# GpSimd normalises two of four tiles, late passes and selection move, and the odd layer's values follow two heads' scores later

## The chip, the cores and the metric

The kernel runs on one core of one Trainium2 chip. The metric is the device time of one execution in microseconds (us), given as the median of several runs. The rows below come from one profiled execution. The engines are named as the profile names them: PE (TensorE, matmuls), PEld (its weight loads), DVE (VectorE), ACT (ScalarE), POOL (GpSimd) and SP (SyncE, which issues most DMAs).

## The reference, cut to what matters

Three blocks act one after the other on 512 tokens of width 1024, in float32.

```
h = rms_norm(x, mix_norm_g)
u, q, k, v, f_logit, g_ssm, g_att = split(h @ w_in)
merged = sigmoid(g_ssm) * s5_branch(u, ...) + sigmoid(g_att) * forgetting_attention(q, k, v, ...)
x = x + merged @ w_out
h2 = rms_norm(x, ffn_norm_g)
x = x + peer_ffn(h2, ...)   # top 16 experts of 16384 per token and head: gelu(h.u) * gate, times v
# even layer: rmsnorm, dsa_mixer (an index scores keys, top_k keeps 128 per token) beside diff_mixer (4 heads), output product
x = x + swiglu(rmsnorm(x, g0), w_gate0, w_up0, w_down0)
# odd layer: rmsnorm, nsa_mixer (16 heads in 4 groups, compressed, selected and windowed keys), output product
x = x + swiglu(rmsnorm(x, g1), w_gate1, w_up1, w_down1)
# diff_mixer, one head:
a = softmax(q0 k0) - lam * softmax(q1 k1);  o = rmsnorm(a @ v) * gain
```

## The kernel before, in words

The 512 tokens are four tiles of 128 rows (`NT = 4`); the width is eight blocks of 128 (`KD = 8`). Each float32 operand is split into a high part and a remainder, and each product is three matmuls, high by high, high by remainder, remainder by high (`mm3`, L332 to L334).

Weights pass through one ordered stream of 1024-column blocks (`Stream`, L56 to L95). A block is loaded by SP into `wraw` (three buffers), its high part `whi` is made by ACT (L75), its remainder `wlo` by DVE (L81); for the names in `ADDED` the remainder is made by an ACT copy of minus w (L78) and a POOL DMA that adds w (L79).

`norm_T` (L323 to L326) makes each normalised tile `xn` on DVE, transposes it on PE into `tx` or `ax`, and ACT and DVE split that into `hhi` and `hlo`. `proj_T` multiplies a weight block by all 512 tokens; `proj_256` gives 256 output columns for each tile.

The stages run in this order, by the profiled execution's time: start norm, `u`, forget gates and the fox attention with the S5 branch in the background (0 to 282 us), gates and output (to 469), norm and peer queries with the top 16 (to 530), the peer passes (530 to 1767), the even layer's norm and index (to 1862), four diff heads with the selection of keys (to 2013), eight latent heads with the output product (to 2126), ffn0 (to 2500), the odd layer (2500 to 2900), ffn1 (to the end). In the peer part there are 128 passes over u and 128 over v. The first `N_SPILL` u passes do not need v; `N_LATE` of them run after the gates are built (ACT, DVE and PE build these from L1106 to L1138 and send them to `gst`, `at`), and the others are mixed with the v passes. Each v pass needs loads of the gates (`g<-gt`, `a<-at`, L1193) and POOL's product `w` (L1200).

The order on each engine is fixed when the kernel is built, by a scheduler that simulates the tile program. Work in the background is written as generators, stepped by `yield_bg`. The selection of the even layer is one: for three tiles, 16 rounds of MAX8 (L1493) and MATCH_REPLACE8 (L1494) on DVE, 96 operations. `diff_second` writes a head's rms norm (`ssd`, then twelve small DVE operations `rv`, `rt`, `ry`, L262 to L269, then `on`, L1555), transposes `on` and leaves it in `oT`. `lat` heads load `uk` and `uv` (L1611 to L1618).

Attention heads run through `pipeline`: `first` of an item makes its scores and exponentials (`pd` or `prow`), `second` divides them (`normalise`, L1323; in the odd layer L1877 to L1882), transposes them (`tx`) and multiplies by the values (`po`):

```
for first, second in items:
    q.append((second, first()))
    between()
    if len(q) > 1:
        g, x = q.pop(0)
        g(x)
```

In the odd layer an item is one head with one of two sets of keys, 32 items in all, and `prep` makes a group's keys and compressed scores `cs` ahead.

## Time and profile before

| What | Value |
|---|---|
| median of 3 runs | 3279.72 us (3277.26 to 3280.32) |
| the profiled execution: its own time, its span | 3279.84 us, 3278.1 us |
| its mean granted TensorE clock | 0.978 |
| PE busy, DVE busy, ACT busy, POOL busy | 3128.9, 2108.7, 1519.0, 709.5 us |

The span runs from the first to the last instruction; 1.7 us of the execution's time lie around it. A granted clock of 1 is 2.4 GHz, of 0.5 it is 1.2 GHz; the mean says that some stretches ran at the lower level. PE's busy share is high, so the time that it stands idle, by stage, and what ended each wait, is what to look at.

### The profile page before, as it was taken

The numbers are of one execution on the slowest core, as the hardware profiler recorded it, in microseconds if no ns is written. First come the engines' busy times: TensorE is split into PE (matmuls) and PEld (weight loads), VectorE is DVE, ScalarE is ACT, GpSimd is POOL, SyncE is SP. The second block draws the span as 40 slices with busy tenths as digits, with TensorE's granted clock in tenths as the row PEclk, the third lists the DMA queues.
The fourth block names the chain that finished last, engine by engine and source line by source line (L and its number), as shares of the span: only waits on it lengthen the run. The fifth ranks groups of instructions, "written<-read, shape, count | busy, mean of one in ns | idle before, by whom it ended". The sixth has DMA issues, their size and how long they took to land.

```text
span 3278.1 us, 46646 instructions
## 1 busy us (share of the span) xinstructions
PE 3128.9 (95%) x17107; PEld 2742.3 (84%) x17107; DVE 2108.7 (64%) x4643; ACT 1519.0 (46%) x2966; POOL 709.5 (22%) x873
## 2 busy tenths in 40 slices
PE   7999999999989999999999986999999998999999
PEld 6998878999988878999998975878888986778887
DVE  6786349999757778887885686643324388743323
ACT  4555233559963333333335664632222378732222
POOL 1561000020015554666662310000000110000000
PEclk9999999999999999999999997999999999999999
DMA  6553232476779998999997641122233210123332
GB/s 177 142 136 115 97 116 84 153 247 243 258 271 342 340 342 300 343 336 324 345 335 205 146 107 42 43 90 97 96 97 124 84 46 10 49 73 98 98 92 83
DMA packets 232758, 551.28 MB, mean 168 GB/s; under 512 B 19785, under 2 KB 113865, under 8 KB 230609
## 3 DMA queue, kind: packets, MB, share of 16 engines
q1 hardware_dynamic: 184432, 349.58, 32.1%
q0 software_dynamic: 43776, 159.40, 15.6%
q10 hardware_dynamic: 4320, 39.32, 3.1%
q8 instruction: 134, 2.20, 0.3%
q14 instruction: 96, 0.78, 0.1%
HBM read 472.60 MB, written 49.82 MB: 159 GB/s over the span
## 4 chain that ended last, share of the span: by engine, by line
PE 81%; DVE 10%; ACT 3%; DMA 3%; issue 2%; POOL 0%; SPq 0%; DVEq 0%; POOLq 0%; ACTq 0%
PE mm L332 21%; PE mm L333 21%; PE mm L334 21%; PE ax L334 2%; PE ax L332 2%; PE ax L333 2%; PE ax L1137 2%; DMA wraw<-in_peer_v_dram 1%; DVE wlo L81 1%; PE tx L1317 1%; PE tx L1887 1%; PE po L1897 1%; DVE xn L323 1%; DVE tl L276 1%; ACT whi L75 1%
## 5 line engine op out<-in xcount | busy, mean ns | idle before, releaser
L75 ACT CAST whi<-wraw 128x1024 fp32r<-128x1024 f32 x525 | 549.2, 1048 | 880.1 <-PE mm L333 325.2
L81 DVE TENSOR_TENSOR wlo<-wraw,whi 128x1024 fp32r<-128x1024 f32 x477 | 600.2, 1258 | 544.0 <-ACT whi L75 537.1
L334 PE MATMUL mm<-hhi,wlo 128*128 128x512 f32 (+1 forms) x1544 | 577.8, 374 | 2.6 <-DVE wlo L81 2.6
L332 PE MATMUL mm<-hhi,whi 128*128 128x512 f32 (+1 forms) x1544 | 577.3, 375 | 0.0
L333 PE MATMUL mm<-hlo,whi 128*128 128x512 f32 (+1 forms) x1544 | 577.2, 374 | 0.0
L332 PE MATMUL mm<-whi,hhi 128*128 128x256 f32 (+1 forms) x1280 | 382.1, 300 | 8.1 <-ACT hhi L275 3.9
L333 PE MATMUL mm<-wlo,hhi 128*128 128x256 f32 (+1 forms) x1280 | 382.4, 299 | 2.0 <-DMA wlo<-wraw 2.0
L334 PE MATMUL mm<-whi,hlo 128*128 128x256 f32 (+1 forms) x1280 | 380.3, 299 | 0.0
L334 PEld LDWEIGHTS mm<-hhi,wlo 128*128 128x128 f32 x1544 | 290.1, 188 | 43.3 <-DVE wlo L81 3.2
L332 PEld LDWEIGHTS mm<-hhi,whi 128*128 128x128 f32 x1544 | 290.4, 188 | 41.4 <-ACT hhi L275 0.7
L333 PEld LDWEIGHTS mm<-hlo,whi 128*128 128x128 f32 x1544 | 290.1, 188 | 40.7 <-DVE hlo L276 0.2
L333 PE MATMUL mm<-wlo,wth 128*128 128x512 f32 x768 | 303.5, 395 | 0.1
L334 PE MATMUL mm<-whi,wtl 128*128 128x512 f32 x768 | 302.5, 394 | 0.0
L979 POOL DMA_INDIRECT rw<-in_peer_rows_dram,idx x128 | 159.9, 1249 | 562.4 <-DVE act L988 339.5
L332 PE MATMUL mm<-whi,wth 128*128 128x512 f32 x768 | 257.6, 397 | 9.4 <-ACT whi L75 9.3
L332 PEld LDWEIGHTS mm<-whi,hhi 128*128 128x128 f32 x1280 | 248.4, 194 | 15.6 <-ACT hhi L275 4.1
L333 PEld LDWEIGHTS mm<-wlo,hhi 128*128 128x128 f32 x1280 | 248.3, 194 | 8.9 <-DMA wlo<-wraw 2.2
L334 PEld LDWEIGHTS mm<-whi,hlo 128*128 128x128 f32 x1280 | 247.2, 194 | 5.9
L1203 ACT CAST wth<-w 128x384 fp32r<-128x384 f32 x128 | 65.7, 514 | 354.9 <-POOL w L1200 209.7
L979 POOL DMA_INDIRECT rw<-in_peer_v_dram,idx x128 | 184.8, 1444 | 113.9 <-DVE acc L996 84.0
L988 DVE CUSTOM_DVE_ANT_0 rw<-rw,hrow 128x1024 f32<-128x1024 f32 x128 | 179.5, 1411 | 9.5 <-DMA rw<-in_peer_rows_dram,idx 9.5
L996 DVE SCALAR_TENSOR_TENSOR acc<-rw,act,acc 128x1024 f32<-128x1024 f32 x127 | 173.8, 1369 | 12.7 <-DMA rw<-in_peer_v_dram,idx 12.0
(567 smaller groups left out, 6111.5 us busy)
## 6 DMA issues: line engine op xcount, KB each, us to landing
wraw<-in_peer_u_dram SPq DMA_DIRECT2D x128, 512.0 KB
wraw<-in_peer_v_dram SPq DMA_DIRECT2D x128, 512.0 KB
wlo<-wraw POOLq DMA_DIRECT2D x48, 512.0 KB
gt<-gst ACTq DMA_DIRECT2D x12, 2048.0 KB
g<-gt SPq DMA_DIRECT2D x32, 768.0 KB
wraw<-in_w_gate_dram SPq DMA_DIRECT2D x44, 512.0 KB
wraw<-in_w_up_dram SPq DMA_DIRECT2D x44, 512.0 KB
wraw<-in_w_down_dram SPq DMA_DIRECT2D x44, 512.0 KB
```

The source lines that it names most:

```text
L75: self.nc.scalar.copy(hi[:, :w], r[:, :w])
L81: self.last = self.nc.vector.tensor_sub(lo[:, :w], r[:, :w], hi[:, :w])
L276: V.tensor_sub(lo, ps, hi)
L323: V.scalar_tensor_tensor(xn, x[:, o], rs, grow[:, o], op0=ALU.mult, op1=ALU.mult)
L332: PE.matmul(ps, ah, bh, start=start, stop=False)
L333: PE.matmul(ps, ah, bl, start=False, stop=False)
L334: PE.matmul(ps, al, bh, start=False, stop=stop)
L979: G.indirect_dma_start(out=rw, out_offset=None, in_=A[("peer_rows", "peer_v")[m]], in_offset=bass.IndirectOffsetOnAxis(ap=idx[:, k:k + 1], ...
L988: V.tensor_tensor_reduce(rw, rw, hrow, 1.0, 0.0, op0=ALU.mult, op1=ALU.add, accum_out=act[:, k:k + 1])
L996: V.scalar_tensor_tensor(acc0, rw, act[:, k:k + 1], acc0, op0=ALU.mult, op1=ALU.add)
L1137: PE.matmul(ps[:, i * P:(i + 1) * P], o2[:, i], og[:, i], start=True, stop=True)
L1203: S.copy(wh, w)
```

## The change

It has nine parts.

- `N_SPILL` goes from 72 to 76, `DOTS_C` from 28 to 32 and `N_LATE` from 8 to 12: four more u passes stand between the gates and the v passes.
- `ADDED` gains the blocks at the head of six products (`u`, `w_query`, `od_kv`, `gate` and `up`), so fourteen remainders go from DVE to ACT and POOL.
- `proj_T_first` takes the first three products after a norm together and writes each in two halves of 256 tokens, the first half for all three before the second.
- `by_tile` takes the first product of the even and of the odd layer one token tile at a time.
- The odd layer's gain row is loaded before ffn0.
- `normalise` gives the two shorter tiles (128 and 256 columns) to POOL, and the odd layer uses `normalise` too, where two were on DVE and two on ACT.
- In the even layer background steps come one at a time between diff heads instead of three, three follow each `ev_qn` product, and the background is drained later; two of the four parts of the output product (`out_parts`) are issued before the latent heads.
- `uk` and `uv` are loaded by POOL's queue instead of SP's.
- `pipeline` gets a depth; the odd layer uses 2, with three buffers for each `pd`, and its last background work waits for head 10 instead of 9.

```
-N_SPILL = 72
-DOTS_C = 28
-N_LATE = 8
+N_SPILL = 76
+DOTS_C = 32
+N_LATE = 12
...
+ADDED += [(n, m) for n in ("u", "w_query") for m in range(3)] + [("od_kv", 0, kk) for kk in range(2)]
+ADDED += [k for i in range(2) for k in (("gate", i, 0), ("up", i, 0), ("gate", i, 1))]
...
+    def proj_T_first(keys, h):
+        us = [ws.get(k, 2 - i) for i, k in enumerate(keys)]
+        pss = [bank_m() for _ in us]
+        for f in range(2):
+            c = slice(256 * f, 256 * f + 256)
+            for ps, (wh, wl) in zip(pss, us):
+                for k in range(KD):
+                    w = slice(k * P, k * P + P)
+                    mm3(ps[:, c], wh[:, w], wl[:, w], h[0][:, k, c], h[1][:, k, c],
+                        k == 0 and f == 0, k == KD - 1 and f == 1)
+        return pss
...
+        for q in range(NT if by_tile else 0):
+            o = pss[q // 2][:, 256 * (q % 2):256 * (q % 2) + 256]
+            for k in range(KD):
+                wh, wl = us[k // 4]
...
+psu = K["proj_T_first"]([("u", m) for m in range(3)], h)
 psf = mm_T(wfh, wfl, h, 8, KD, 0)
...
 def normalise(K, Ps, fac):
-        if r == NT - 1:
+        if r < 2:
+            nc.gpsimd.tensor_scalar(Ps[r][:, :W], Ps[r][:, :W], fac[:, r:r + 1], None, op0=ALU.mult)
+        elif r == NT - 1:
...
-        if len(q) > 1:
+        if len(q) > depth:
...
-        pipeline(K, diff_heads(), lambda: yield_bg(3))
-        drain_bg()
+        pipeline(K, diff_heads(), yield_bg)
         for m in range(4):
-            stack_even_odd(K, qn[m], proj_T(("ev_qn", m), h))
+            ps = proj_T(("ev_qn", m), h)
+            yield_bg(3)
+            stack_even_odd(K, qn[m], ps)
...
-        bg.append(out_parts())
+        parts = out_parts()
+        for _ in range(6):
+            next(parts)
+            yield_bg(3)
+        drain_bg()
+        bg.append(parts)
...
-            SY.dma_start(raw, src[:, hd * P:(hd + 1) * P])
+            G.dma_start(raw, src[:, hd * P:(hd + 1) * P])
...
-        h = K["norm_T"](lambda t: xr[:, t, :], A["norm_mix"][1:2], xp, state["sums"])
+        h = K["norm_T"](lambda t: xr[:, t, :], state["grow"], xp, state["sums"])
...
-            for r in range(NT):
-                if r % 2:
-                    S.activation(Ps[r], Ps[r], AF.Copy, scale=den[:, r:r + 1])
-                else:
-                    V.tensor_scalar(Ps[r], Ps[r], den[:, r:r + 1], None, op0=ALU.mult)
+            normalise(K, Ps, den)
...
-        pipeline(K, items(), lambda: yield_bg(2))
+        pipeline(K, items(), lambda: yield_bg(2), 2)
```

The first place is DVE at the last two diff heads of the even layer, before the change. `m` and `sel` are the selection, `on` is a head's normed output; the first `on` here is the third head's, the second the fourth's, and `ry` and `rt` are its small steps.

```order
L1493 MAX m_2624_20140<-sel_17971 128x8
L1555 TENSOR_TENSOR on_20031<-po_20019,ry_20037 128x512
L1494 MATCH_REPLACE sel_17969<-m_2622_20134,sel_17969 128x256
L1494 MATCH_REPLACE sel_17970<-m_2623_20137,sel_17970 128x384
L1494 MATCH_REPLACE sel_17971<-m_2624_20140,sel_17971 128x512
...
L262 TENSOR_SCALAR rv_20109<-ssd_20103 128x4
...
L268 SCALAR_TENSOR_TENSOR rt_20123<-rt_20123,rv_20109 128x4
L269 SCALAR_TENSOR_TENSOR ry_20110<-rt_20123,ry_20110 128x4
L1555 TENSOR_TENSOR on_20104<-po_20092,ry_20110 128x512
```

The same place on DVE after the change, just ahead of the fourth head's `on`.

```order
L1527 MATCH_REPLACE sel_18113<-m_2636_20564,sel_18113 128x384
L1526 MAX m_2637_20567<-sel_18114 128x8
L1526 MAX m_2638_20570<-sel_18112 128x8
L271 SCALAR_TENSOR_TENSOR ry_20182<-rt_20191,ry_20182 128x4
L1526 MAX m_2639_20573<-sel_18113 128x8
L1527 MATCH_REPLACE sel_18114<-m_2637_20567,sel_18114 128x512
L1527 MATCH_REPLACE sel_18112<-m_2638_20570,sel_18112 128x256
L269 TENSOR_TENSOR rt_20195<-ry_20182 128x4
...
L1530 TENSOR_SCALAR sel_18114<-sel_18114 128x512
L1588 TENSOR_TENSOR on_20176<-po_20164,ry_20182 128x512
```

Selection operations that stood ahead of the first three heads' `on` now stand between the third's and the fourth's: in the four stretches that end at an `on` there were 38, 35, 20 and 3 of the 96, and there are 26, 8, 13 and 49.

The second place is SP's queue where the v passes begin, before the change. `g` and `a` are gate loads, `wraw` the weights of one pass.

```order
L67 DMA wraw_10938<-in_peer_u_dram 128x1024
L1193 DMA g_10923<-gt 128x12x128
L1193 DMA a_1410_10919<-at 128x1536
L1193 DMA g_10925<-gt 128x12x128
L447 DMA xr<-x_sc_5467 128x1024 x4
L67 DMA wraw_10976<-in_peer_u_dram 128x1024
L1193 DMA g_11242<-gt 128x12x128
L67 DMA wraw_11014<-in_peer_v_dram 128x1024
```

The same place on SP after the change.

```order
L1223 DMA g_11079<-gt 128x12x128
L1223 DMA a_1412_11075<-at 128x1536
L1223 DMA g_11081<-gt 128x12x128
L69 DMA wraw_11094<-in_peer_u_dram 128x1024
L475 DMA xr<-x_sc_5543 128x1024 x4
L1223 DMA g_11534<-gt 128x12x128
L69 DMA wraw_11132<-in_peer_u_dram 128x1024
...
L1223 DMA g_11806<-gt 128x12x128
L69 DMA wraw_11300<-in_peer_v_dram 128x1024
```

The first v weights stood right behind the second group of gate loads; now six u blocks stand between, and one u block that stood ahead of the gate loads stands behind them. On PE, six u passes followed the last gate transposes before the first v matmul, and now eleven do.

The third place is PE at the norm ahead of ffn1, before the change. `ax<-ident,xn` are the transposes, `mm` the first products.

```order
L326 MATMUL ax_28528<-ident,xn_28526 128x128 x4
...
L326 MATMUL ax_28600<-ident,xn_28598 128x128 x4
L326 MATMUL ax_28609<-ident,xn_28607 128x128 x4
L332 MATMUL mm_28634<-hhi_28518,whi_28432 128x512
L332 MATMUL mm_28667<-hhi_28518,whi_28622 128x512
```

The same place on PE after the change.

```order
L328 MATMUL ax_28808<-ident,xn_28806 128x128 x4
L334 MATMUL mm_28868<-hhi_28750,whi_28663 128x256
L334 MATMUL mm_28869<-hhi_28750,whi_28854 128x256
L334 MATMUL mm_28870<-hhi_28750,whi_28859 128x256
L328 MATMUL ax_28817<-ident,xn_28815 128x128 x4
L335 MATMUL mm_28868<-hlo_28751,whi_28663 128x256
...
L328 MATMUL ax_28841<-ident,xn_28839 128x128 x4
```

All eight groups of transposes stood ahead of the first product; now half products stand between them, 26 ahead of the last tile's, and on DVE no remainder of a weight block stands among the steps of this norm.

## Rows read from the trace of the kernel before

**Rows 1.** Part 1 of the page, busy time of each engine.

```profile
PE 3128.9 (95%) x17107; PEld 2742.3 (84%) x17107; DVE 2108.7 (64%) x4643; ACT 1519.0 (46%) x2966; POOL 709.5 (22%) x873
```

**Rows 2.** PE's waits: us, times, longest. Whole span; last 2900:2905, 2500:2509.

```profile
PE tx L1317 <- DVE on L1555: 30.5, 3, 13.3
PE ax L326 <- DVE xn L323: 15.2, 5, 5.1
PE tx L326 <- DVE xn L323: 14.9, 3, 7.5
PE mm L332 <- ACT whi L75: 9.3, 3, 7.1
PE mm L1659 <- ACT uk L1617: 7.3, 1, 7.3
...
PE mm L333 <- DMA wlo<-wraw: 2.0, 1, 2.0
...
PE ax L326 <- DVE xn L323: 4.8, 1, 4.8
...
PE tx L326 <- DVE xn L323: 5.2, 1, 5.2
```

**Rows 3.** Stretches: length, PE, PEld, DVE, ACT, POOL busy, clock, DMA share, GB/s.

```profile
2896.00:2908.00 12.00, 6.93 (x39) 5.83 (x37) 11.94 (x23) 7.02 (x16) 0.00 (x0) 0.72 0.26 87
...
1862.00:2013.00 151.00, 106.81 (x689) 97.32 (x688) 118.45 (x349) 82.63 (x195) 24.16 (x34) 0.82 0.36 92
2013.00:2126.00 113.00, 105.23 (x635) 91.64 (x636) 73.77 (x186) 67.79 (x168) 3.13 (x6) 0.98 0.13 41
...
2640.00:2880.00 240.00, 223.37 (x1351) 178.87 (x1350) 190.59 (x562) 187.56 (x500) 11.71 (x14) 0.95 0.10 34
```

**Rows 4.** Chain of waits at ffn1's norm: start us, us, what.

```profile
2898.97 1.14 DVE wlo L81
...
2900.18 1.12 DVE wlo L81
```

**Rows 5.** Chain of waits at the odd layer's norm.

```profile
2502.06 4.41 DMA grow<-in_norm_mix_dram
```

**Rows 6.** PE's groups by form, 947.6 to 972.9: busy us, mean ns, idle.

```profile
L332 PE MATMUL ax<-hhi,whi 128*128 128x384 f32 x48 | 16.1, 336 | 0.0
```

**Rows 7.** Chain of waits where the v passes begin.

```profile
964.35 14.39 DMA wraw<-in_peer_v_dram
```

**Rows 8.** Chain of waits at the selection and the first latent head.

```profile
1982.28 1.38 DVE m L1493 x3
...
1988.68 1.58 DVE sel L1494 x4
...
2006.10 6.97 DMA uk<-in_ev_w_uk_dram
```

**Rows 9.** Groups of 2640 to 2880 by form: busy us, mean ns, idle.

```profile
L1880 ACT ACTIVATE pd<-pd,den 128x512 f32<-128x512 f32 x31 | 22.1, 714 | 0.0
...
L1880 ACT ACTIVATE pd<-pd,den 128x256 f32<-128x256 f32 x31 | 15.7, 505 | 1.5 <-DVE den L1877 1.4
...
L1882 DVE TENSOR_SCALAR pd<-pd,den 128x128 f32<-128x128 f32 x31 | 9.8, 315 | 0.6
...
L1295 POOL TENSOR_TENSOR rb<-rx,s 128x256 f32<-128x256 f32 x10 | 9.2, 946 | 27.5 <-ACT rx L1292 22.7 <-DVE krow L1789 2.9 <-DVE den L1877 1.9
...
L1799 POOL COPY kdup<-krow 128x512 f32<-128x512 f32 x4 | 2.5, 614 | 80.4 <-PE tx L1317 78.5 <-DVE krow L1789 1.9
```

**Rows 10.** Chain of waits in ffn1, one matmul of 512 columns.

```profile
2908.87 0.23 PE mm L333
```

**Rows 11.** Chain of waits in the even layer's first product, one matmul of 256 columns.

```profile
1781.19 0.12 PE mm L332
```

**Rows 12.** Chain of waits from the forget gates to the first fox head.

```profile
45.34 5.01 DMA cre<-in_ssm_c_re_dram
...
77.66 0.44 DVE qn L882
```

More of the change, by code (lines that the diff above doesn't have):

```diff
@@ L36 @@
 TOPK = 16
-ADDED = ("w_kq", "w_v", "ev_a", "ev_iq", "ev_qk", "ev_vb", "ev_qn")
+ADDED = ["w_kq", "w_v", "ev_a", "ev_iq", "ev_qk", "ev_vb", "ev_qn"]
+ADDED += [(n, m) for n in ("u", "w_query") for m in range(3)] + [("od_kv", 0, kk) for kk in range(2)]
+ADDED += [k for i in range(2) for k in (("gate", i, 0), ("up", i, 0), ("gate", i, 1))]
 def pool_in(tc, **kw):
@@ L75, in _split @@
         self.nc.scalar.copy(hi[:, :w], r[:, :w])
-        if self.specs[i][0][0] in ADDED:
+        if self.specs[i][0] in ADDED or self.specs[i][0][0] in ADDED:
             self.nc.scalar.activation(lo[:, :w], r[:, :w], AF.Copy, scale=-1.0)
@@ L368, in proj_row, with proj_256 @@
         return pss
-    def proj_256(key, h, c0, nk=KD, tick=2, k0=0):
+    def proj_256(key, h, c0, nk=KD, tick=2, k0=0, by_tile=False):
         pss = [bank_m() for _ in range(2)]
-        for kk in range(k0 // 4, nk // 4):
+        if by_tile:
+            us = [ws.get((key, c0, kk), 1) for kk in range(2)]
+        for q in range(NT if by_tile else 0):
+            o = pss[q // 2][:, 256 * (q % 2):256 * (q % 2) + 256]
+            for k in range(KD):
+                wh, wl = us[k // 4]
+                c = slice(k % 4 * 256, k % 4 * 256 + 256)
+                mm3(o, h[0][:, k, q * P:(q + 1) * P], h[1][:, k, q * P:(q + 1) * P], wh[:, c], wl[:, c],
+                    k == 0 and q % 2 == 0, k == KD - 1 and q % 2 == 1)
+        for kk in range(k0 // 4, 0 if by_tile else nk // 4):
             wh, wl = ws.get((key, c0, kk))
@@ L423, in body @@
         if 4 + 2 * layer in phases:
+            if layer == 0 and 5 in phases:
+                state["gain"] = ExitStack()
+                state["grow"] = load_gain(A["norm_mix"][1:2], state["gain"].enter_context(
+                    pool_in(tc, name="gain", bufs=1)))
             if layer == 1 and 7 in phases:
@@ L828, in mixer1 @@
         for m in range(4):
-            ps = proj_T(("u", m), h)
+            ps = psu[m] if m < 3 else proj_T(("u", m), h)
             ut = sp1.tile([P, 4, P], F32, name="ut", tag="y4")
@@ L1028, in peer @@
                 SY.dma_start(keys, A["sub_keys"])
+                psq = K["proj_T_first"]([("w_query", m) for m in range(3)], h)
                 for m in range(16):
-                    ps = proj_T(("w_query", m), h)
+                    ps = psq[m] if m < 3 else proj_T(("w_query", m), h)
                     qt = qp.tile([P, T], F32, tag="qt", bufs=2, name=nm("qt"))
@@ L1268, in ffn @@
         al = fp.tile([P, NF, T], F32R, name="al")
+        first = K["proj_T_first"]([("gate", i, 0), ("up", i, 0), ("gate", i, 1)], h)
         for m in range(NF):
-            pg = proj_T(("gate", i, m), h)
+            pg = first.pop(0) if first else proj_T(("gate", i, m), h)
             sg = fp.tile([P, T], F32, tag="sg", bufs=3, name=nm("sg"))
             S.activation(sg, pg, AF.Silu)
-            pu = proj_T(("up", i, m), h)
+            pu = first.pop(0) if first else proj_T(("up", i, m), h)
             V.tensor_mul(sg, sg, pu)
@@ L1357, in causal_mask, with pipeline @@
     return mk
-def pipeline(K, items, between):
+def pipeline(K, items, between, depth=1):
     q = []
@@ L1416, in even_mixer @@
         qr = ep.tile([P, NT, 8, 32], F32, name="qr")
-        pss = proj_256("ev_a", h, 0)
+        pss = proj_256("ev_a", h, 0, by_tile=True)
         for t in range(0, NT, 2):
@@ L1559, in diff_heads @@
             for hd in range(4):
-                pss = proj_256("ev_qk", h, 256 * hd)
+                pss = proj_256("ev_qk", h, 256 * hd, tick=1)
                 qrow = dpl.tile([P, NT, 2, 64], F32, tag="qrow", bufs=1, name=nm("qrow"))
@@ L1577, in diff_heads @@
                 if hd < 2:
-                    pss = proj_256("ev_vb", h, 256 * hd)
+                    pss = proj_256("ev_vb", h, 256 * hd, tick=1)
                     for t in range(0, NT, 2):
@@ L1689, in odd_mixer @@
     with pool_in(tc, name="ox", bufs=1) as xp:
-        h = K["norm_T"](lambda t: xr[:, t, :], A["norm_mix"][1:2], xp, state["sums"])
+        h = K["norm_T"](lambda t: xr[:, t, :], state["grow"], xp, state["sums"])
+    state["gain"].close()
     x_sc = park_res(K, state)
@@ L1717, in odd_mixer @@
             crow = [qp.tile([P, NT, 4, 2, 64], F32, name=f"crow{i}") for i in range(2)]
-            pss = proj_256("od_kv", h, 0)
+            pss = proj_256("od_kv", h, 0, by_tile=True)
             for t in range(0, NT, 2):
@@ L1845, in prep @@
                 pes.close()
-                while at[0] < 9:
+                while at[0] < 10:
                     yield
@@ L1866, in first @@
                 PE.matmul(ps[:, :N], qr, kl[:, :N], start=False, stop=True)
-                p = op.tile([P, W], F32, tag=f"pd{r}", bufs=3 if r > 1 else 2, name=nm("pd"))
+                p = op.tile([P, W], F32, tag=f"pd{r}", bufs=3, name=nm("pd"))
                 V.tensor_tensor_reduce(p, ps[:, :W], mk[:, T - W:], -1.0, 3.0e38, op0=ALU.add, op1=ALU.min,
```

## The prediction

> **What bounds the kernel now.** I read the busy times first [rows 1]: PE is busy 3128.9 of 3278.1 us, and the other engines have at least a third of the span to spare. So the whole prize is PE's 149 us of idle time, and whatever the lower clock costs. Second come PE's waits [rows 2]. They are few and local: 30.5 us for three `on` of the diff heads, 15.2 and 14.9 us for normalised tiles `xn` (4.8 at ffn1's norm, 5.2 at the odd layer's), 9.3 us for weights, 7.3 us for `uk`. Third, the stretches [rows 3] tell how a stage with such a wait looks: in the diff heads (1862 to 2013) PE works 106.8 of 151 us at a mean clock of 0.82, while DVE works 118.5. Stages with long waits thus pay twice, since the matmuls behind a wait run at the lower level for a while. I do not price that second part by itself; it is a reserve inside the range.
>
> **The change part by part.** All sums are against the profiled execution, 3279.84 us, which is 0.12 us from the median.
>
> *Price of the halves.* A matmul of 512 columns takes 0.23 us in the chain [rows 10] and one of 256 takes 0.12 [rows 11]. The 288 added matmuls replace 288 long ones by pairs: 288 x 0.01 = +2.9 us, or 0.7 for each of four places. I count it inside the terms below.
>
> *Norms ahead of the peer queries and the two ffns.* At ffn1's norm PE worked 6.93 of 12 us [rows 3]. DVE was full for 11.94 of them, and two of its steps, 1.14 and 1.12 us, are the remainders of weight blocks [rows 4], in front of `hlo` and of the last tiles. Both go to ACT and POOL, so `hlo` and the third tile come some 2.3 us earlier; and 26 half products now stand ahead of the last tile, 3.1 us of work at 0.12, where PE waited. ACT pays: a copy for each remainder, about as long as DVE's step, stands ahead of its own `hhi`. Of the wait of 4.8 us (5.1 is the longest of its kind) I take 3 as gained each time, net of the halves: 3 x -3 = -9. Bounds: 0 if the remainder made by DMA comes late (below), -4 each if the whole wait goes.
>
> *Norms of the even and the odd layer.* At the odd one the gain row's DMA of 4.41 us [rows 5] stood alone in the chain until `xn` could start. It goes ahead of ffn0, and what is late next is the root of the row sums and a DVE remainder; `by_tile` then starts the product after one tile. -4, between -2 and the 5.2 us that PE idled. At the even norm only the tile order helps: -2, between 0 and -4.
>
> *Start.* The three `u` products start with the first two tiles and win some 3.5 us. But the forget gates now stand behind them on PE. From the gates a chain runs over the SP queue to the state-space loads (`cre` lands at 45.34 + 5.01 = 50.35) and through DVE to the first head's `qn` at 77.66 [rows 12], where PE already waits. In the order the gates' matmuls stood among the first 40 on PE and stand behind 144 half ones now, some 10 us later. DVE has 149 instead of 186 instructions between the gates and `qn`, 37 fewer; at 27.3 us for 186 that is 0.15 each, 5.5 back. So `qn` comes some 3 to 4 us late, and PE has about 1.5 us more done by then: +1 in all, between -4 and +6.
>
> *Late passes.* Six u passes follow the last gate transposes, 144 matmuls (three lines of 48) in 25 us without idle time [rows 6], so 4.2 us each. Then PE waited 7.1 us for weights [rows 2]: SP's queue stands at the gate loads until POOL has used the first, and only then the first v weights are asked for, at 964.35, and take 14.39 us [rows 7]. They land at 978.7. Now eleven passes stand there, 21 us more work, so v is no longer late. What is late next is a u block: the eighth pass's weights stand at the same place of the queue, behind the second gate loads, and are wanted at 947.6 + 7 x 4.2 = 977. Landing at 978.7 and a split behind it, that is a wait of 3 us. The gain is the 9.3 us of the three such waits [rows 2] less 3, so -6. Bounds: 0 if the u block waits as long as v did, -9.
>
> *Selection later.* A round of three MAX8 takes 1.38 and three replacements 1.58 us [rows 8], 0.49 an operation. The order gives 38, 35, 20 and 3 operations in the four stretches before, 26, 8, 13 and 49 after. Second `on`: 27 operations less are 13 us, the wait of 13.3 falls to about 3, as PE then gets there with little to spare. Third: 7 less, but PE has only some 7.6 us of work for 18 on DVE, so the wait is about 11 to 13. Fourth: 49 operations are 24 us, with `on`'s own small steps and the masks 29, against 4 us of PE work: 25. The third and fourth now are 30.5 - 13.3 = 17.2 together [rows 2]. The wait for `uk`, 7.3 us, goes, for its DMA of 6.97 [rows 8] no longer stands behind four loads on SP, and some 9 us of PE work lie between the fourth `on` and its use. Waits: 30.5 + 7.3 = 37.8 before, 3 + 13 + 25 = 41 after, +3. In return two output parts, 96 matmuls of 256 columns, 11.5 us, are done before the latent heads: -8 in all at their start. These parts filled gaps there; PE idled 7.8 of 113 us [rows 3], and I add half of it again: +4. Sum -4, between -15 (DVE, 118.5 of 151, gives no waits of its own) and +8 (the fourth wait costs all that the second saves, and the heads miss their filler).
>
> *Odd layer, depth two and GpSimd.* Between 2640 and 2880 PE idled 16.6 us; ACT worked 187.6 and DVE 190.6 of 240 [rows 3]. ACT loses 32 scalings of 505 ns, 16 us, DVE 32 of 315, 10 us [rows 9]. With depth two the end of a chain of scores has a whole head's set of matmuls in front of it, so the waits for `pd`, `tf` and `tl`, and the last one with no scores left to do, shrink; those for `cs` do not. -6, between -14 and +10.
>
> GpSimd's scalings are not in the trace. A POOL copy of 512 columns takes 614 ns, a two-input product of 256 columns 946 [rows 9]. Two in a row, of 128 and 256 columns, then take 0.7 to 1.5 us; I take 1.1. The longest other scaling is ACT's 714 ns. So a head's tiles come some 0.4 us later, and depth two gives 3 us of cover. The latent heads have depth one; I count that in their +4.
>
> A rule speaks against this edit. The Trainium skill, "GPSIMD Engine Reference", section 4.1 Engine selection, wants elementwise work on VectorE, with GpSimd about twice as slow for two inputs and about line-rate for one. The trace agrees that one input is far cheaper there (1.2 ns a column in the copy, 3.7 in the product [rows 9]). By its one-input part the scalings are hidden and the sum stays; by its two-input part the rival of late scalings below would cost its 38 us.
>
> Sum: +1 - 9 - 6 - 6 - 4 - 6 = -30, so 3279.84 - 30 = 3250.
>
> **The rivals.** *The stall only moves in the even layer.* DVE stands full until the fourth `on`, so its wait could be longer than 25 us, and the latent heads have no filler: the term is +8, the time 3262. For it speaks that the same 96 operations are done by the same engine; against it that DVE idled 32 of 151 us. Chance 0.16.
>
> *More than that.* The diff stage closes to what DVE needs (-15) and the odd layer's idle time nearly goes (-14): 3250 - 11 - 8 = 3231. For it speaks that DVE and ACT are under 80% busy in the odd stage. Chance 0.18.
>
> *GpSimd is late.* `normalise` is called 48 times (8 fox heads, 8 latent, 32 items). If POOL takes 1.5 us where 0.7 sufficed, and it also issues DMAs and rope products in line, each transposition waits up to 0.8 us: 38 us, on a forecast without the odd layer's gain, 3256 + 38 = 3294, slower than before. It decides from 24 / 48 = 0.5 us exposed at each call on. Against it: POOL works 11.7 of 240 us there. Chance 0.09.
>
> *Remainders land late.* A remainder made through DMA was once waited for 2.0 us [rows 2]; at three norms that is +6: 3256, inside the forecast's band. The Trainium skill, "DMA: Bandwidth & Descriptors", section on the anatomy of a SWDGE DMA, fits 2.0 us plus the bytes by 436 GB/s; by that an estimate for 512 KB is 3.2 us from issue, against 1.1 for the DVE step. Nothing in the sum uses it.
>
> **How the numbers follow.** Forecast 0.57 (3240 to 3263 by itself), the moved stall 0.16, more 0.18, late GpSimd 0.09. The range 3229 to 3272 leaves out late GpSimd and the outer parts of the two others, and takes in the bounds of single terms. A measurement here can tell 0.2%, 6.6 us: faster means under 3273. Faster holds for the forecast, for the rival with more, and for nearly all of the moved stall: 0.86. Same is 0.06, between it and late GpSimd, slower 0.08.
>
> **What would show it.** Right: no wait at `uk`; one long wait, over 20 us, for the fourth `on`, and under 5 for the second; no wait over 4 us before the v passes; PE's idle time at the three norms under 2.5 us; POOL scalings of 1.1 us a pair. Wrong: PE waits for POOL's `pd` or `prow` tens of times, a wait over 6 us at the first fox `qn`, or a wait for `wlo` by DMA behind each norm. The prediction falls if the diff heads and latent heads together end more than 8 us later than by the terms above.

## The result, and the profile after

The changed kernel took 3295.14 us (median of 7 runs, 3290.74 to 3303.13) where the kernel before took 3279.72 (3276.57 to 3286.36 beside them): ratio 1.0052, 95% interval 1.0043 to 1.0062. It is slower by about 17 us; 30 less was forecast. Its profiled execution took 3299.66 us, span 3297.8, clock 0.979, so 4.5 us above its median. One per mille of the time before is 3.28 us; I compare kernels by their ratios to the kernel before, which ran beside each of them.

Busy time of each engine (page, part 1), to be held against [rows 1]:

```profile
PE 3134.0 (95%) x17395; PEld 2758.1 (84%) x17395; DVE 2091.2 (63%) x4565; ACT 1519.4 (46%) x2948; POOL 800.5 (24%) x999
```

PE has 5 us more work and 15 us more idle time. PE's waits over the whole span (us, times, longest), beside [rows 2]:

```profile
PE tx L1348 <- DVE on L1588: 41.8, 3, 20.2
PE ax L334 <- ACT as L1204: 13.2, 2, 12.9
PE tx L328 <- DVE xn L325: 11.0, 3, 7.7
PE mm L334 <- ACT hhi L277: 8.2, 3, 3.9
PE mm L334 <- ACT whi L77: 8.0, 6, 2.9
PE ax L328 <- DVE hlo L278: 5.2, 2, 2.6
PE mm L334 <- ACT ut L860: 4.5, 2, 3.1
...
PE mm L335 <- DMA wlo<-wraw: 4.2, 2, 3.7
...
PE tx L841 <- POOL st L776: 2.9, 1, 2.9
...
PE tx L1372 <- POOL pd L1358: 2.4, 2, 1.9
```

What was meant to go did go: the waits of `ax` for `xn` (15.2 us) are no longer there, two of 2.6 us for `hlo` stand at the two ffns, one of 2.7 us for `hhi` (of the 8.2) at the peer norm, and no wait for `uk` is left. The second line is new: 12.9 us in one piece for `as`, ACT's result of a late u pass.

Stretches, as in [rows 3]: the first three lie in the late passes, then the diff heads, the latent heads, the odd layer and ffn1's norm.

```profile
962.00:992.00 30.00, 16.76 (x95) 15.94 (x93) 11.54 (x11) 9.47 (x16) 9.42 (x8) 0.82 1.03 356
992.00:995.00 3.00, 3.00 (x10) 3.00 (x11) 0.00 (x0) 0.27 (x1) 0.00 (x0) 0.51 0.75 216
995.00:1015.00 20.00, 20.00 (x116) 19.87 (x115) 4.90 (x4) 6.49 (x9) 1.16 (x1) 1.00 0.54 190
...
1899.00:2049.00 150.00, 106.14 (x707) 97.83 (x706) 114.24 (x329) 76.53 (x190) 21.36 (x33) 0.84 0.33 88
2049.00:2156.00 107.00, 98.02 (x534) 80.52 (x534) 66.44 (x169) 67.39 (x169) 21.26 (x29) 0.97 0.15 45
2661.00:2901.00 240.00, 221.14 (x1365) 178.77 (x1364) 187.51 (x535) 177.37 (x472) 66.78 (x79) 0.96 0.10 34
2919.20:2931.20 12.00, 9.43 (x69) 9.14 (x68) 9.36 (x18) 8.20 (x16) 1.71 (x2) 0.86 0.74 180
```

At ffn1's norm PE works 9.43 of 12 us instead of 6.93. In the odd layer ACT is 10 us lighter than before and PE does 2.2 us less in the same 240 us.

The chain of waits through the late passes (start us, us, what):

```profile
957.80 0.17 PE ax L336
...
962.07 10.47 DMA wraw<-in_peer_u_dram
972.63 1.06 ACT whi L77
...
975.57 11.03 DMA a<-at
986.75 4.63 POOL w L1230 x4
991.40 0.50 ACT as L1204
991.94 0.69 PE ax L334
992.63 0.32 PE ax L335
```

To be read backwards: PE went on at 991.94, when ACT had taken a result out of a PSUM bank. ACT could not sooner, for its `as` at 991.40 needed a buffer that POOL's four products were reading until 991.38; and these waited for the load `a<-at`, issued at 975.57, 11 us long. (Of the loads called gate loads above, only `g<-gt` brings gates; `a<-at` brings back the stored results of four earlier u passes.) And PE pays twice: its next matmuls follow each other at 0.32 us, at a granted clock of 0.51 (the lower level) until 995, and at 0.17 before.

To see where the rest went, this table takes from each trace the start of the first PE instruction of each stage; a figure is the us from one such start to the next. "Late" runs from the first u pass behind the gates to the thirteenth, with the same matmuls in each kernel; from there to the even norm it is 447.6 to 448.4 us in all of them, and left out. "Again" is a second profiled execution of the changed kernel; the other columns are kernels of the next section.

| us | before | changed | again | third buffer | eight | both | norms | best |
|---|---|---|---|---|---|---|---|---|
| start to the peer norm | 468.4 | 470.9 | 472.5 | 472.6 | 470.4 | 472.1 | 468.0 | 470.8 |
| to the first late pass | 479.2 | 482.1 | 479.7 | 479.5 | 476.3 | 473.3 | 477.3 | 474.8 |
| late | 368.4 | 383.2 | 381.0 | 366.6 | 367.7 | 365.2 | 368.7 | 366.9 |
| even norm and index | 112.5 | 115.4 | 114.5 | 112.0 | 112.1 | 115.6 | 114.0 | 112.3 |
| diff and latent heads | 252.6 | 256.5 | 255.6 | 259.5 | 257.3 | 256.7 | 255.6 | 252.3 |
| ffn0 to the odd norm | 378.4 | 370.9 | 370.9 | 371.0 | 371.0 | 371.0 | 372.6 | 370.9 |
| odd layer | 389.7 | 392.6 | 388.5 | 391.5 | 385.5 | 389.5 | 391.2 | 387.5 |
| ffn1 | 380.9 | 378.6 | 378.7 | 378.7 | 378.9 | 378.5 | 379.2 | 377.3 |

Late passes: +14.8 us. The two ffn rows: -9.8. The odd layer moves by 4 us between two executions of one kernel, so a few us there say nothing.

### The profile page after: what moved, and what is told of

Its sections match the earlier page's. It is cut to its first block, busy times and chain, and to the rows that moved or that the text cites. A ratio compares the mean times of both kernels' runs of the same rounds, so it can differ in the third digit from the quotient of the medians.

```text
span 3297.8 us, 47395 instructions
## 1 busy us (share of the span) xinstructions
PE 3134.0 (95%) x17395; PEld 2758.1 (84%) x17395; DVE 2091.2 (63%) x4565; ACT 1519.4 (46%) x2948; POOL 800.5 (24%) x999
## 3 DMA queue, kind: packets, MB, share of 16 engines
q0 software_dynamic: 46304, 167.79, 16.8%
## 4 chain that ended last, share of the span: by engine, by line
PE 60%; DVE 5%; DMA 3%; ACT 2%; issue 1%; POOL 0%; SPq 0%; DVEq 0%; ACTq 0%; POOLq 0%
PE mm L334 15%; PE mm L335 15%; PE mm L336 15%; PE ax L334 3%; PE ax L336 3%; PE ax L335 3%; DMA wraw<-in_peer_v_dram 1%; PE tx L1348 1%; PE tx L1923 1%; ACT whi L77 1%; DMA wlo<-wraw 1%; DVE sel L1527 1%; PE po L1933 1%; DVE wlo L83 1%; DVE m L1526 0%
## 5 line engine op out<-in xcount | busy, mean ns | idle before, releaser
L83 DVE TENSOR_TENSOR wlo<-wraw,whi 128x1024 fp32r<-128x1024 f32 x463 | 591.5, 1278 | 562.1 <-ACT whi L77 555.2
L334 PE MATMUL mm<-hhi,whi 128*128 128x512 f32 (+2 forms) x1640 | 597.8, 365 | 6.4 <-ACT hhi L277 4.3
L336 PE MATMUL mm<-hhi,wlo 128*128 128x512 f32 (+2 forms) x1640 | 596.3, 364 | 4.9 <-DVE wlo L83 2.9
L335 PE MATMUL mm<-hlo,whi 128*128 128x512 f32 (+2 forms) x1640 | 598.0, 365 | 0.3 <-DVE hlo L278 0.3
L334 PE MATMUL mm<-whi,hhi 128*128 128x256 f32 (+1 forms) x1280 | 385.2, 303 | 19.0 <-ACT ut L860 4.5
L334 PEld LDWEIGHTS mm<-hhi,whi 128*128 128x128 f32 x1640 | 311.3, 190 | 44.4 <-ACT hhi L277 4.9
L336 PEld LDWEIGHTS mm<-hhi,wlo 128*128 128x128 f32 x1640 | 311.1, 190 | 42.9 <-DVE wlo L83 3.7
L335 PEld LDWEIGHTS mm<-hlo,whi 128*128 128x128 f32 x1640 | 311.4, 190 | 36.6 <-DVE hlo L278 0.5
L1008 POOL DMA_INDIRECT rw<-in_peer_rows_dram,idx x128 | 156.0, 1219 | 571.8 <-DVE act L1017 378.7
L81 POOL DMA_DIRECT2D wlo<-wraw x62 | 54.8, 884 | 755.2 <-ACT wlo L80 740.1
## 6 DMA issues: line engine op xcount, KB each, us to landing
g<-gt SPq DMA_DIRECT2D x32, 768.0 KB, 10.2
```

The costliest lines, as they stand in the source:

```text
L81: self.nc.gpsimd.dma_start(lo[:, :w], r[:, :w], accum_op=ALU.add)
L83: self.last = self.nc.vector.tensor_sub(lo[:, :w], r[:, :w], hi[:, :w])
L334: PE.matmul(ps, ah, bh, start=start, stop=False)
L335: PE.matmul(ps, ah, bl, start=False, stop=False)
L336: PE.matmul(ps, al, bh, start=False, stop=stop)
L1008: G.indirect_dma_start(out=rw, out_offset=None, in_=A[("peer_rows", "peer_v")[m]], in_offset=bass.IndirectOffsetOnAxis(ap=idx[:, k:k + 1], ...
```

## The experiments

### The late passes

**Third buffer** (changed kernel). `as` and `a<-at` share the tag `a4` with two buffers; they get three where the late passes and the v passes use them.

```
-                    state["a4"] = pool.tile([P, 4, TD], F32, tag="a4", bufs=2, name=nm("as"))
+                    state["a4"] = pool.tile([P, 4, TD], F32, tag="a4", bufs=2 if bank is bank_m else 3, name=nm("as"))
...
-                    d[q] = vp.tile(shape, F32, tag=tag, bufs=2 if tag == "a4" else 3, name=nm(tag))
+                    d[q] = vp.tile(shape, F32, tag=tag, bufs=3, name=nm(tag))
```

> The changed kernel with a third a4 buffer in the v part, so that the last four late passes need not wait until the second group of spilled rows has been used. Theory (the two a4 buffers are the cause): the wait of 12.95 us for ACT as goes, what stays is the wait for a u block that the prediction put at 3 us; 3295 - 10 = 3285, and a little more where the clock stays up. Rival (the queue of loads is the cause, the buffer only where it shows): PE waits nearly as long for weights of the next passes, 3292 to 3295.

3280.46 us, ratio 1.0004 (0.9994 to 1.0014): 15.7 us less than the changed kernel. ACT's timeline of the changed kernel shows the hole (start us, us, ..., idle before and releaser):

```profile
974.00 0.48 ACT L1204 ACTIVATE as<-ax 128x384 f32<-128x384 f32 x1
...
991.40 0.87 ACT L1204 ACTIVATE as<-ax 128x384 f32<-128x384 f32 x2 [2.02 <-POOL w L1230]
```

Four results fill the first buffer, the last at 974.00; the fifth and sixth wait till 991.40. The two `ax` banks are full by then, and PE stands. In the kernel before, ACT took the fifth and sixth while POOL's second four products were still running, so it did not wait for these (its copy of the last of them, `wth`, starts only at 985.57, when that product ends):

```profile
983.43 0.86 ACT L1174 ACTIVATE as<-ax 128x384 f32<-128x384 f32 x2
985.57 0.51 ACT L1203 CAST wth<-w 128x384 fp32r<-128x384 f32 x1 [1.27 <-POOL w L1200]
```

With a third buffer the fifth no longer waits for POOL, and PE's waits from 940 to 1020 have no `as` in them. What is left is a wait for weights just ahead of the eighth pass, the one that the prediction put at 3 us:

```profile
PE ax L334 <- ACT whi L77: 3.6, 1, 3.6
```

**Eight late passes** (changed kernel with `N_SPILL` 72, `DOTS_C` 28, `N_LATE` 8).

> The changed kernel with N_SPILL 72, DOTS_C 28 and N_LATE 8 as before. Theory (late passes are the largest loss, 14 us between the first late pass and the even layer's norm): 3295 - 14 = 3281, and the wait ahead of the v passes is one of some 7 us for whi again. Rival (the loss there comes from other parts, such as loads that now compete): 3288 or more.

3269.23, ratio 0.9971 (0.9959 to 0.9984): 26.6 us less, 11 more than the buffer explains. The v passes wait for weights as they did before: from 940 to 1020 there is

```profile
PE mm L334 <- ACT whi L77: 7.3, 1, 7.3
```

**Both** (changed kernel, third buffer, `DOTS_C` 28, twelve late passes).

> The changed kernel with the third a4 buffer, twelve late passes kept, and DOTS_C back at 28. The third buffer alone gave 3280.5; undoing all three constants gave 3269.2. Theory (the four added late passes cost nothing once they have a buffer, and what remained between those two kernels is the row steps that DOTS_C 32 asks for ahead of the gates): about 3274, within 3271 to 3277, with the first late u pass about 4 us earlier than with the buffer alone. Rival (the order of the late passes itself costs, DOTS_C is neutral): 3279 to 3282.

3271.27, ratio 0.9975 (0.9964 to 0.9987): 9.5 us less than the buffer alone. `DOTS_C` is the number of gathered rows (POOL's gather, a dot product on DVE) spread over the first `N_SPILL` passes. From 540 to 952 us, with 32, in the third-buffer kernel:

```profile
540.00:952.00 412.00, 403.58 (x2527) 393.15 (x2526) 367.96 (x1211) 302.21 (x673) 33.23 (x27) 0.99 0.61 213
```

and with 28:

```profile
540.00:952.00 412.00, 406.26 (x2564) 395.95 (x2563) 364.83 (x1202) 303.61 (x676) 30.44 (x24) 1.00 0.59 214
```

Three gathers and 3.1 us of DVE less, in the stage in which DVE makes the gates; the late passes begin 6.7 us earlier. This undoes a little more than the change did: ahead of the first late pass 25 rows are gathered in the kernel before (28 over 72 passes), 27 in the changed one (32 over 76) and 24 here (28 over 76). Against eight late passes there is no difference to be told (0.9975 and 0.9971): passes moved ahead of v have a wait to fill, but it is no longer worth 9 us, for the `late` row falls by 2.5 us only.

**`DOTS_C` 28 with two buffers** (changed kernel).

> The changed kernel with DOTS_C at 28 and nothing else undone: two a4 buffers and twelve late passes. With a third buffer DOTS_C was worth 9.2 us. Theory (a buffer's wait and the row steps add up): 3295.1 - 9.2 = 3286. Rival (PE would only reach the wait for the buffer sooner, and wait that much longer): 3293 to 3296.

3282.78, ratio 1.0024 (1.0012 to 1.0036): 9.2 us less. The wait for `as` is 12.9 us again, so the two costs add: `DOTS_C` is worth 9.2 and 9.5 us, with two buffers and with three, and the third buffer 15.7 and 16.1 (1.0024 to 0.9975), with `DOTS_C` 32 and 28.

**The three constants on the kernel before.**

> The kernel before with the three constants of the late passes alone (N_SPILL 76, DOTS_C 32, N_LATE 12). Theory (two buffers for a4 are too few for a third group of late passes, and DOTS_C 32 is late by some us): 3279.7 + 14 to 20, so about 3297, with one wait of PE for ACT's as of about 13 us. Rival (the stall only appears together with the other parts, as they make the gates late): 3276 to 3284.

3287.19, ratio 1.0029 (1.0019 to 1.004): +9.5, under the expected. The stall is there:

```profile
PE tx L1317 <- DVE on L1555: 15.6, 3, 9.6
...
PE ax L332 <- ACT as L1174: 11.9, 1, 11.9
```

By stages, the late passes last 378.4 us, 10.0 more than in the kernel before (14.8 more in the changed kernel), and the stage ahead of them 479.1 against 479.2: the `DOTS_C` rows cost nothing there. The first of these lines shows another thing: the diff heads, where no code was changed, wait 15.6 us for `on` and not 30.5. The scheduler sets the order anew for a changed program, and the waits of the selection came out otherwise; their stage is 3.4 us shorter.

**The constants with the norm parts** (on the kernel before).

> The kernel before with the norm parts and with the three constants of the late passes. The norm parts alone gave 3270.3, the constants alone cost 8.1. Theory (the two are independent): 3278.4, within 3275 to 3282. Rival (the wait for the a4 buffer grows when PE and DVE come earlier from the norms, so that what the norms gain is waited for there): 3284 to 3292.

3284.2, ratio 1.0025 (1.0015 to 1.0035). The norm parts alone stand at 0.9969 (below), so the constants cost 18 us here. The time is the rival's, its reason is not, for the wait for `as` has hardly grown:

```profile
PE tx L1347 <- DVE on L1585: 30.5, 3, 13.3
PE ax L334 <- ACT as L1203: 13.8, 2, 12.4
...
PE mm L335 <- DMA wlo<-wraw: 7.1, 3, 4.1
```

**The changed kernel again.**

> The changed kernel once more, for its trace. In its first trace the odd stage lasted 392.6 us from the norm to the next norm, and kernels with the same code there lasted 385.5 to 392. If these differences are run to run, a second trace shows the odd stage some us off 392.6; if they come with the order that was built, it shows 392 to 393 again. The wait for the a4 buffer should be 12 to 14 us again in both cases.

One run, 3291.39 us. The `as` wait is 12.9 again; the odd layer lasts 388.5 us, not 392.6. So that part of the difference was run to run.

```profile
PE ax L334 <- ACT as L1204: 13.5, 2, 12.9
```

### The norms

**The norm parts alone** (kernel before with halves at the peer queries, ffn0 and ffn1, their remainders by DMA, the product by tile, the gain row ahead of ffn0).

> The kernel before with the norm parts alone: the halves at the peer queries and the two ffns with their remainders by DMA, the first product by tile in the even and the odd layer, and the gain row loaded ahead of ffn0. By the prediction's terms these are -9 - 2 - 4 = -15, so 3265. By the profile of the changed kernel the idle time at ffn0 and ffn1 fell by 2 to 4 us each, the even norm's did not change, and the odd norm still waits for a remainder: about -9, so 3271. Rival (the remainders by DMA land late and eat it): 3276 or more.

3270.3, ratio 0.9969 (0.9957 to 0.9981): -10.2. PE's waits from 2495 to 2535 show what is left of the odd norm, with the DMA remainder late:

```profile
PE mm L335 <- DMA wlo<-wraw: 2.6, 1, 2.6
PE tx L328 <- DVE hlo L278: 1.6, 1, 1.6
PE tx L328 <- DVE xn L325: 1.4, 1, 1.4
```

### The start

**Old start** (changed kernel).

```
-ADDED += [(n, m) for n in ("u", "w_query") for m in range(3)]
+ADDED += [(n, m) for n in ("w_query",) for m in range(3)]
...
-psu = K["proj_T_first"]([("u", m) for m in range(3)], h)
...
-ps = psu[m] if m < 3 else proj_T(("u", m), h)
+ps = proj_T(("u", m), h)
```

> The changed kernel with the start as before: no proj_T_first for u, u's remainders on DVE. Theory (the forget gates behind the u products cost 4.4 us by the end of the fox attention): 3291, and the wait at the first fox qn is back while those for ut go. Rival (the 4.4 us come from POOL's scalings in the fox heads or elsewhere): 3295.

3291.14, ratio 1.0035 (1.0023 to 1.0046). The total and the waits are as expected (the transposes wait for `qn` again and nothing for `ut`), the place is not: the peer norm begins at 471.9 us, no earlier than in the changed kernel. In these traces the largest gain lies in the odd layer (385.2 us against 392.6 and 388.5), which the edit does not touch. PE's waits up to 284 us still have

```profile
PE tx L840 <- POOL st L775: 3.0, 1, 3.0
PE tx L1347 <- DVE qn L910: 2.9, 1, 2.9
```

The wait for `st`, POOL's part of the S5 branch, was 0.5 us in the kernel before; it is 2.5 us with the new start and without GpSimd's scalings too (a kernel below), so either edit alone brings it.

### The selection

**Old selection** (changed kernel: three background steps between diff heads and two, not one, behind each weight block of their products, drained before `ev_qn`, `out_parts` whole behind it).

```
-pss = proj_256("ev_qk", h, 256 * hd, tick=1)
+pss = proj_256("ev_qk", h, 256 * hd)
...
-pipeline(K, diff_heads(), yield_bg)
+pipeline(K, diff_heads(), lambda: yield_bg(3))
+drain_bg()
...
-parts = out_parts()
-for _ in range(6):
-    next(parts)
-    yield_bg(3)
-drain_bg()
-bg.append(parts)
+bg.append(out_parts())
```

> The changed kernel with the selection and the output parts as before (three background steps between diff heads, all drained before ev_qn), uk and uv still on POOL's queue. Theory (moving the selection only moved the stall and took the latent heads' filler: +5.7 us over both stages, while uk's queue alone would win 5 to 7): 3283 to 3289, the waits for on 13, 12 and 5 us again and none for uk. Rival (the loss is POOL's prow scalings in the latent heads): 3295, with waits on POOL pd or prow in the latent heads still.

3288.57, ratio 1.0033 (1.002 to 1.0045): 6 us less. The waits for `on` are not the 30 us of the kernel before; other waits stand in the diff heads instead (1896 to 2027):

```profile
PE tx L1348 <- DVE on L1588: 16.4, 3, 9.5
PE sx L1550 <- DVE mx L1554: 5.5, 3, 4.3
PE sx L1550 <- DVE qs L1341: 5.0, 1, 5.0
```

**Old selection on eight late passes.**

> The kernel with 8 late passes (e2, 3269) and the selection and output parts as before. Theory (the two losses are in separate stages and add): 3269 - 6.6 = 3262.6. Rival (part of the 6.6 us of e4 came from elsewhere, the odd stage above all): 3266 to 3269.

3266.75, ratio 0.9962 (0.995 to 0.9974): 3 us less than eight late passes, between theory and rival and inside the intervals. Here the order has 30.1 us of waits for `on` again. The selection's new place gains nothing in either; it costs 3 to 6 us, each at or within the intervals.

### The odd layer and GpSimd

**Depth one** (changed kernel).

```
-pipeline(K, items(), lambda: yield_bg(2), 2)
+pipeline(K, items(), lambda: yield_bg(2))
...
-while at[0] < 10:
+while at[0] < 9:
```

> The changed kernel with depth 1 in the odd layer (and the last background work at head 9). Theory (depth two hides GpSimd's scalings, which take 760 and 1018 ns there instead of the 1.1 us a pair I had; without it each of 32 items waits for pd): 3295 + 10 to 20 = 3305 to 3315, with waits of PE tx for POOL pd in most items. Rival (depth two brings nothing, as the odd stage waits for scores' maxima and for tl): 3293 to 3297.

3290.05, ratio 1.0038 (1.0024 to 1.0052): 4.6 us less, under theory and rival both. PE waits for POOL's `pd` no more than in the changed kernel (2.4 us, twice), so depth two hid nothing of these scalings.

**Depth two on the kernel before**, with three buffers for each `pd`.

> The kernel before with depth 2 in the odd layer alone (three buffers for each pd, last work at head 10), scalings as before on DVE and ACT. Theory (depth two alone shortens the waits for pd, tf and the last one, the scalings on GpSimd give that back): 3279.7 - 5 = 3275. Rival (DVE's and ACT's own pace bounds the odd stage, depth moves only which wait shows): 3279.

3282.5, ratio 1.0012 (1.0003 to 1.0021): 3.9 us more, over theory and rival both. Both ways round, depth two costs about 4 us, each time at the edge of the intervals.

**Eight late passes without GpSimd in `normalise`.**

```
-if r < 2:
-    nc.gpsimd.tensor_scalar(Ps[r][:, :W], Ps[r][:, :W], fac[:, r:r + 1], None, op0=ALU.mult)
-elif r == NT - 1:
+if r == NT - 1:
```

> The kernel with 8 late passes (e2, 3269) and normalise without GpSimd, so three tiles on DVE and one on ACT in all three attentions. Theory (POOL's scalings delay its state-space products in the fox heads, 4 us by the gelu, and its prow and pd in the latent heads, 2.4 us, and gain nothing in the odd layer): 3263. Rival (they relieve DVE in the odd layer, where it is at 78%): the fox heads win 4 and the odd layer loses 10, 3275.

3288.38, ratio 1.0031 (1.002 to 1.0041): 19.7 us more than eight late passes. The theory, that GpSimd's scalings are of no use, falls, and the rival is right for the odd layer alone. Of the 20 us, 9.9 lie ahead of the peer norm (480.3 against 470.4) and 8.4 in the odd layer (393.9 against 385.5). Without GpSimd's help, from 2640 to 2880:

```profile
2640.00:2880.00 240.00, 224.07 (x1402) 182.49 (x1401) 202.16 (x612) 178.40 (x478) 15.39 (x18) 0.96 0.10 34
```

and with it:

```profile
2640.00:2880.00 240.00, 222.63 (x1357) 179.28 (x1356) 184.94 (x526) 179.41 (x475) 62.97 (x75) 0.97 0.10 33
```

DVE is at 202 of 240 us when it has three of the four tiles. In the odd layer that is one tile more than in the kernel before, so this alone does not price the edit; the last kernel below does.

**Best of the parts** (eight late passes, old selection, depth one; norms, start, GpSimd's scalings and the loads of `uk` and `uv` by POOL's queue stay).

> The changed kernel with eight late passes and the old constants, the selection at its old places, and depth one in the odd layer: the norms, the start, GpSimd's scalings and the POOL loads of uk and uv remain. Eight late passes with the old selection gave 3266.8; depth one gave 5 us on the changed kernel. Theory (the three parts are independent): 3262, within 3258 to 3265. Rival (depth one only gained through the order that the other parts left): 3265 to 3270.

3262.99, ratio 0.9952 (0.9938 to 0.9966): the fastest of all, 15.7 us under the kernel before. Its waits are those of the kernel before at the selection and at v, and that for `uk` is down from 7.3 to 1.3 us. The diff and latent heads together are no shorter for it (252.3 us against 252.6):

```profile
PE tx L1348 <- DVE on L1588: 30.0, 3, 13.1
...
PE mm L334 <- ACT whi L77: 8.4, 2, 7.1
```

**Best with the odd layer's scalings back** on ACT and DVE, two tiles each.

> The kernel with eight late passes, old selection and depth one, 3263.0, and with the odd layer's scalings back on ACT and DVE, two tiles each. Theory (GpSimd's pair of 1.76 us is longer than the longest scaling elsewhere, so it delays 32 items and gains little, as DVE and ACT are not full there): 3259 to 3263. Rival (DVE and ACT need the relief, as they did when all scalings were taken back and the odd stage lost 8 us): 3267 to 3272.

3265.83, ratio 0.9968 (0.9956 to 0.998): 5 us more by the ratios, 2.8 by the medians, between theory and rival, and with intervals that overlap. From 2625 to 2865, with the scalings back:

```profile
2625.00:2865.00 240.00, 223.54 (x1396) 180.51 (x1396) 194.49 (x580) 191.38 (x512) 13.13 (x17) 0.96 0.11 36
```

and on GpSimd:

```profile
2625.00:2865.00 240.00, 223.94 (x1412) 181.69 (x1412) 192.05 (x551) 183.32 (x483) 68.28 (x81) 0.98 0.11 36
```

The odd layer lasts 390.9 and 387.5 us. Against my theory GpSimd's scalings are, if anything, a gain there; more is not shown.

## Why the prediction was wrong

The way from the kernel before to the changed one, by kernels that differ in one part each (in the second step in three), is: norm parts -10.2; start, GpSimd's scalings and POOL's loads of `uk` and `uv` together -5.6 (0.9969 to 0.9952); depth two +3.3 (to 0.9962); selection +3.0 (to 0.9971); late passes +26.6 (to 1.0052). Each step is uncertain by some 5 us, from the intervals, so only the first and the last are clear of zero, and the loads of `uk` and `uv` were never tried alone. Without the last the kernel would have been faster by 9.5 us.

**The step that failed is "Late passes", -6.** I followed the queue of weights and forecast a wait of 3 us at a u block. That was right as far as it went: with the third buffer PE waits 3.6 us for weights ahead of the eighth pass. But I named no buffer for what the passes write. The step of the argument that broke is "what is late next is a u block": next, ahead of the seventh pass, is the `a4` buffer. Late results and the loads `a<-at` share two; in the changed order the second of these loads and POOL's four products on it come ahead of the second group of results, which has to wait for them: 12.9 us of PE idle, then 3 us at the lower clock. (Where the expectations speak of the third group, the trace shows the second, the fifth result on.) The third buffer gave back 15.7 and 16.1 us. The gain was too large besides: waits for `whi` are 8.1 us in all with the third buffer (4.5 and 3.6) and 8.0 with two, against 9.3 before, so some 1 us went and not 6. And `DOTS_C` was left out of the working altogether, an edit costed at nothing with no cover named: 9 us by two pairs of kernels for three rows, two of which the change had added. In the kernels with the norm parts the stage ahead of the late passes follows the rows: 473.3 and 475.0 us with 24, 474.8 to 477.6 with 25, 478.6 to 482.1 with 27. On the kernel before it does not (479.2 with 25, 479.1 with 27), so why a row costs some 2 us there, at 1 us of DVE, is not shown.

**"Selection later", -4, was wrong in its account.** I forecast 41 us of waits for `on` (3, 13, 25) and none for `uk`; measured are 41.8 (9.8, 11.9, 20.2) and none. That the sum agrees is luck: the second wait is 7 us longer than forecast, the fourth 5 shorter. But then I took 8 us back for two output parts "done before the latent heads". Moved work is no saved work: the diff stage grows by what the latent stage loses. Without that credit the account is the waits, +3 by forecast and 41.8 - 37.8 = +4.0 as measured; the table's row has +3.9, and undoing the edit gave 3 to 6 us. The row is 7.9 us over the term, just under the 8 us at which I had said the prediction falls. The rival of the moved stall had this mechanism, and its price was too high.

**"Odd layer", -6.** Depth two was to cover the waits of 16.6 us of idle time and costs 3 to 5 us instead, in three pairs of kernels (4.6, 3.9, 3.3). The step that failed is that the waits for `pd`, `tf` and `tl` shrink: in the changed kernel those for `tl` in the odd layer are 4.8 us (2.5 and 2.3), with depth one 1.0. That they are what depth two costs is not shown, for the stage varies by 4 us by itself. GpSimd's pair is longer than I took (2661 to 2901):

```profile
L1358 POOL TENSOR_SCALAR pd<-pd,den 128x256 f32<-128x256 f32 x32 | 32.6, 1018 | 0.0
L1358 POOL TENSOR_SCALAR pd<-pd,den 128x128 f32<-128x128 f32 x31 | 23.4, 754 | 150.4 <-DVE den L1917 40.5 <-ACT th L277 37.5 <-PE tx L1923 35.0
```

1.77 us, not 1.1, over the upper bound of 1.5, and 1.06 longer than ACT's 714 ns. Had that been exposed at each call, the late GpSimd rival ("from 0.5 us") would have come true. It did not: PE waits for POOL's `pd` twice, 2.4 us, both in the latent heads, and as much with depth one in the odd layer. Why the pair stays hidden even so was not looked into. The Trainium skill, "GPSIMD Engine Reference", section 4.1 Engine selection, has GpSimd about line-rate for one input; the measurement is otherwise, 754 ns against DVE's 315 for 128 columns [rows 9]. The kernel is no slower for it (0.9952 with the odd layer's scalings on GpSimd, 0.9968 without).

**"Norms", -9 and -4 and -2.** Right in kind: -10.2 for -15. At ffn0 and ffn1 the waits fell from 5.1 to 2.6 us each, and at the peer norm from 5.1 to 3.0, for -3 forecast. The gain row's wait went (ffn0's row of the table fell by 7.5, 2.5 of it at its own norm), but the odd product then waited for a DMA remainder (3.7 us in the changed kernel, 2.6 in the norm parts), the rival "remainders land late" at this one place. The estimate of 3.2 us for such a DMA was low: by part 6 of the changed kernel's page, the 62 of them took 5.2 us from issue to landing (the median).

```profile
wlo<-wraw POOLq DMA_DIRECT2D x62, 512.0 KB, 5.2
```

The even norm gained nothing: it had waited for `hhi`, 3.9 us, and still does.

**"Start", +1.** The peer norm begins 2.5 and 4.1 us later in the two traces of the changed kernel. Either edit alone delays it too: with the old start and GpSimd's scalings it begins 3.5 us late, with the new start and without the scalings 12 (480.3). The way I had named, a late `qn` that PE's transposes wait for, is not what shows: that wait was 2.6 us and is gone, and 4.5 us for `ut` stand instead. Where the 12 us come from was not traced. In five kernels with neither edit this row lies between 464.8 and 468.4, so the smaller figures may be the order of the build alone.

**What stays open.** The three constants cost 9.5 us alone, 18 on the norm parts and 26.6 in the changed kernel. The stall is 12 to 13 us in each. By the traces, the late passes and the stage ahead of them together grow by 9.9, 14.8 and 21.3 us (16.8 in the second execution of the changed kernel), and why by such different amounts is not explained. The rest, -5.0, -1.4 and +9.7 (+5.9), lies in stages that the constants do not touch, where the build orders the program anew (waits for `on` of 15.6, 30.5 and 41.8 us) and where the odd layer varies by 4 us between executions; I could not part the two.

## What to carry to other kernels

When more work is moved ahead of a wait, ask for each tile that it writes which buffers it takes, who else holds them, and when they let go: the weights were covered and the results were not. Work that is moved counts at both ends, at its new place as well as its old one; only the waits that it fills are gained. And a constant that comes along in the diff needs its own line in the sum.

## What the runs showed of the hardware

- GpSimd's scaling by a column of factors took 754 ns for 128 columns and 1018 for 256 in the odd layer; its copy of 512 took 614 [rows 9]. In the fox heads the same two scalings took 994 and 937, so the width alone does not give the time:

```profile
L1358 POOL TENSOR_SCALAR prow<-prow,den 128x128 f32<-128x128 f32 x8 | 8.0, 994 | 49.8 <-DVE den L888 48.6 <-DVE t L712 1.2
L1358 POOL TENSOR_SCALAR prow<-prow,den 128x256 f32<-128x256 f32 x8 | 7.5, 937 | 0.0
```

- The load `a<-at`, 128x1536 (768 KB), took 11.03 us from issue to landing in a stretch where the DMA share was 1.03 by the profile and 356 GB/s were moved.
- Behind the 12.9 us wait PE ran for 3 us at a granted clock of 0.51, with a matmul of 384 columns each 0.32 us instead of 0.17.
